# The Fourier half of an encoder kernel in tiles of 128 by 128 alone

## Chip, cores, metric

The kernel runs on one core of a Trainium2 chip. The metric is the device time of one execution in microseconds. Matrix products run on TensorE (PE), elementwise work on VectorE (DVE), ScalarE (ACT) and GpSimd (POOL); loads and stores are issued from SyncE's queue (SP).

## What is computed

Two layers of an encoder, on one sequence of 512 positions with 1024 channels, all in fp32. The reference, cut to what matters:

```python
h = rmsnorm(x, norm1[l])
p = h @ w_in[l]                       # columns: u (512) | q (512) | k (128) | v (128)
f = jnp.fft.fft2(u, axes=(1, 2), norm="ortho").real
y_f = f @ w_fourier[l] + b_fourier[l]
y_a = windowed_gqa(rope(rmsnorm(q)), rope(rmsnorm(k)), v, sink[l])   # 8 heads, |i-j| <= 128
x = x + concat([rmsnorm(y_f), rmsnorm(y_a)]) @ w_o[l]
h = rmsnorm(x, norm2[l])
up = dwconv_centred(h @ w_up[l], conv_w[l], conv_b[l])
x = x + (silu(gate) * val) @ w_down[l]
```

The edit is in the Fourier line and the product behind it.

## The kernel before

x stays on chip, transposed: eight tiles of 128 channels by 512 positions. Each layer projects q, k and v, then does the Fourier half and the attention interleaved, then the output product and the feed-forward part. In layer 0 the Fourier half runs on plain fp32 operands: one call of `mm3` is one product in the code (line 118), which the trace shows as two instructions. In layer 1 (and everywhere in the feed-forward part) each operand is split into a high and a low fp32r half, and `mm3` issues three products: high by high, low by high, high by low (lines 120 to 122). The split is `split`: ACT writes the high half (line 90), DVE the low half (line 93, or line 96 with a scale).

The Fourier half uses the symmetry of a real transform. `fold` turns 512 columns into sums (columns 0 to 256, the even plane, the last being the alternating row, sum of x[n](-1)^n) and differences (columns 257 to 511, the odd plane). So the even plane has 257 rows, in tiles of 128, 128 and 1, and the odd plane 255, in tiles of 128 and 127. The program has four steps:

- the up-projection: over eight k tiles, products into `pee[0..2]` (even) and `poo` (odd);
- stage one and stage two (`for stage in range(2)`): products with the cosine and sine tables `tabs` along channels, then along positions. The 257th row is carried apart, in `tail`, and its part is added by a product with the alternating vector `alts`, one row high (lines 589 and 591);
- between them `stage_out`, which copies the sums from PSUM into `slab` tiles and the 257th row into `tail`;
- the product with the Fourier weights, folded by `fold_wf` from `w_fold`, for four column blocks j. The weight row 256 (`wtr`, `wt`) is a product one row high.

The order of instructions on every engine is set by the framework's scheduler from its own timing of the program, so an edit of shapes may also move other work. Each engine works through its list in that order, and waits on semaphores for what the others make. In layer 0 the weights of the Fourier half are folded on DVE when they are loaded; those of layer 1 are folded and split ahead, during the feed-forward part of layer 0 (`presplit`), and fetched (`fetch`). The tables come by `load_tables`: straight into place for layer 0, and through a temporary tile of the group `m4` (five buffers) with a split for layer 1.

Among the work around the change, three names matter below. `kss` and `qs` are the rotated k and q (tiles shown as `m`), which PE transposes (lines 475 and 464). `qk3r` is a reciprocal root for twelve head pairs that POOL makes by a power (line 210), and `qknr` a DVE step on it (line 428). `ropetab` are the rotary tables, multiplied on DVE by the norm weights once a layer. L506, L510 and L518 are the scores, the masked row maximum and the transposes of the attention.

Of the kernel before, what the change touches and what calls it, by code (L numbers as in the profile page):

```python
# [16 lines left out]
P = 128  # L17
# [20 lines left out]
def encoder_kernel(tc, t):  # L38
# [34 lines left out]
    TEMPS = {"act": (1024, 8), "m4": (1024, 5), "slab": (1028, 4), "pT": (2560, 2),  # L73
# [75 lines left out]
    def presplit(l):  # L149
# [33 lines left out]
        for j in range(NF):  # L183
            jobs.append((lambda j=j: [wload(t["w_fold"][l, j], 1024, temp(1024, "m4"))], [f"f{j}"]))
# [97 lines left out]
    def load_tables(l):  # L282
        tab = []
        for i in range(2):
            if l:
                raw = temp(512, "m4")
                nc.sync.dma_start(raw, t["dft"][i])
                tab.append([cp.tile([P, 512], F32R, tag=f"t{z}{i}", name=nm("tab")) for z in "hl"])
                split(*tab[i], raw)
            else:  # L290
                tab.append([cp.tile([P, 512], F32, tag=f"th{i}", name=nm("tab"))])
                nc.sync.dma_start(tab[i][0], t["dft"][i])
        alt = cp.tile([1, 258], F32R if l else F32, tag="altr", name=nm("altr"))
        if l:
            raw = temp(258, "m4")[:1]
            nc.sync.dma_start(raw, t["alt"])
            act(alt, raw)
        else:
            nc.sync.dma_start(alt, t["alt"])
        return tab, alt  # L300
# [35 lines left out]

    def fold_wf(raw, w=None):
# [15 lines left out]
    for l in range(L):  # L353
# [205 lines left out]
        def tail_out(pe, scale):  # L559
# [4 lines left out]
        def stage_out(pe, po, scale):  # L564
            tiles = []
            if not l:
                two = temp(1028, "slab")
            for m in range(2):
                a = halves(pair("slab", 514)) if l else [two[:, m * 514:(m + 1) * 514]]
                n = P - m  # L570
# [3 lines left out]
            return tiles, tail_out(pe, scale)  # L574

        ue, ut = stage_out(pee, poo, 1.0)
        for stage in range(2):
            pe = [psum(), psum(), psum("sc")]
            po = psum()
            for m, (c0, c1) in enumerate(((0, 128), (128, 256), (256, 257))):  # L580
                o = pe[m][:c1 - c0, :258]
                for i in range(2):
                    if stage == 0:
                        mm3(o, [z[:, c0:c1] for z in ue[i]], [z[:, 0:258] for z in tabs[i]], i == 0, False)
                    else:
                        mm3(o, [z[:, c0:c1] for z in tabs[i]], [z[:, 0:258] for z in ue[i]], i == 0, False)
                for z in ut:
                    if stage == 0:
                        nc.tensor.matmul(o, z[:, c0:c1], alts, start=False, stop=z is ut[-1])
                    else:  # L590
                        nc.tensor.matmul(o, alts[:, c0:c1], z, start=False, stop=z is ut[-1])
            for m in range(2):
                n = P - m
                o = po[:n, m * 256:(m + 1) * 256]
                for i in range(2):
                    kn = P - i
                    u2 = [z[:kn, 258:514] for z in ue[i]]
                    t2_ = [z[:kn] for z in tabs[i]]
                    st = m == 0 and i == 0
                    if stage == 0:  # L600
                        mm3(o, [z[:, 1 + m * P:1 + m * P + n] for z in u2], [z[:, 256:512] for z in t2_],
                            st, i == 1, skip_group_check=True)
                    else:
                        mm3(o, [z[:, 257 + m * P:257 + m * P + n] for z in t2_], u2,
                            st, i == 1, skip_group_check=True)
# [9 lines left out]
        for j in range(NF):  # L615
# [9 lines left out]
            else:  # L625
                wt = [wtr]
                w = [fold_wf(wload(t["w_fold"][l, j], 1024), wwhole())]
# [3 lines left out]
            mm3(pu[:, :258], wt, ut, False, True)  # L631
            for i in range(2):
                kn = P - i
                mm3(pv[:, :256], [z[:kn] for z in wsum[2 + i]],
                    [z[:kn, 258:514] for z in ue[i]], i == 0, i == 1)
# [204 lines left out]
```

## Time and profile before

| | |
|---|---|
| runs | 1074.64, 1075.63, 1077.24 us; median 1075.63 |
| profiled execution | 1076.12 us, span 1074.3 us, granted clock 0.998 |
| layer 0: Fourier half and attention | about 46 to 165 us |
| layer 1: the same | about 583 to 690 us |
| HBM traffic | 131 GB/s over the span |

Times in the profile are microseconds from the first instruction. "Span" is first to last instruction; the execution's own time has 1.8 us more around it. A row of the chain or timeline gives the start, the length and what ran; "[idle <-who]" is idle time of that engine ahead of the row and what ended it. An `xN` merges N instructions of a kind. Rows of the chain follow ends, rows of the timeline starts, so the same instruction stands some tenths apart in the two. Shapes like `128*1 128x258` give the stationary operand's rows*columns and the moving operand's rows x columns.

### The profile page before, as it was taken

How to read it: one execution, taken by the hardware profiler on the slowest of the kernel's cores; microseconds unless marked ns; L12 is line 12 of the kernel's file. 1: busy time of each engine (PE TensorE's matmuls, PEld its weight loads, DVE VectorE, ACT ScalarE, POOL GpSimd, SP SyncE). 2: the span in 40 equal slices, each digit the busy share in tenths (PEclk: the TensorE clock that was granted, in tenths of full speed). 3: DMA queues.
4: the chain of work that ended last, by engine and by line, in shares of the span. 5: the costliest groups of instructions: out<-in, count | busy, mean ns of one | idle time of the engine just before them, and what ended most of it. 6: DMA issues, size and time to landing. Idle time of an engine off the chain costs nothing.

```text
span 1074.3 us, 14345 instructions
## 1 busy us (share of the span) xinstructions
PE 1060.8 (99%) x5075; PEld 881.9 (82%) x5075; DVE 737.2 (69%) x1364; ACT 510.4 (48%) x940; POOL 118.4 (11%) x171
## 2 busy tenths in 40 slices
PE   8999999999999999999999999999999999999998
PEld 7866888888888888888899887888888888888887
DVE  7856767697767777776619788387887336777632
ACT  5338755454544445455414775155554224444421
POOL 1134410000000000000001442001211000101000
PEclk9999999999999999999999999999999999999999
DMA  7242162333259932338856322423332333233241
GB/s 276 83 138 84 36 196 79 99 98 98 86 174 372 367 99 97 99 104 297 299 182 212 112 70 79 138 79 99 98 99 81 101 106 100 85 102 94 81 147 47
DMA packets 58859, 142.13 MB, mean 132 GB/s; under 512 B 6554, under 2 KB 19108, under 8 KB 58788
## 3 DMA queue, kind: packets, MB, share of 16 engines
q1 hardware_dynamic: 58788, 141.22, 40.3%
q8 instruction: 40, 0.66, 0.3%
q14 instruction: 31, 0.25, 0.1%
HBM read 118.12 MB, written 23.07 MB: 131 GB/s over the span
## 4 chain that ended last, share of the span: by engine, by line
PE 92%; DVE 4%; ACT 1%; DMA 1%; issue 1%; SPq 0%; POOL 0%; DVEq 0%; ACTq 0%
PE ps L120 27%; PE ps L122 27%; PE ps L121 27%; PE ps L118 5%; PE ps L506 2%; PE ps L518 2%; DMA wraw<-in_w_qkv_dram 1%; DVE act L93 1%; PE ps L224 1%; DVE tF L96 1%; PE ps L217 1%; DVE tA L510 0%; PE ps L464 0%; DVE tF L93 0%; DVE slab L93 0%
## 5 line engine op out<-in xcount | busy, mean ns | idle before, releaser
L90 ACT ACTIVATE whi<-wraw 128x512 fp32r<-128x512 f32 (+1 forms) x296 | 181.9, 616 | 297.8 <-PE ps L122 281.4
L93 DVE TENSOR_TENSOR wlo<-wraw,whi 128x512 fp32r<-128x512 f32 (+1 forms) x304 | 221.9, 732 | 115.5 <-ACT whi L90 113.9
L120 PE MATMUL ps<-act,whi 128*128 128x512 f32 x768 | 298.9, 390 | 0.0
L121 PE MATMUL ps<-act,wlo 128*128 128x512 f32 x768 | 298.7, 389 | 0.0
L122 PE MATMUL ps<-act,whi 128*128 128x512 f32 x768 | 298.4, 389 | 0.0
L122 PEld LDWEIGHTS ps<-act,whi 128*128 128x128 f32 x768 | 144.2, 188 | 29.9
L121 PEld LDWEIGHTS ps<-act,wlo 128*128 128x128 f32 x768 | 144.2, 188 | 29.9
L120 PEld LDWEIGHTS ps<-act,whi 128*128 128x128 f32 x768 | 144.2, 188 | 29.8
L96 DVE SCALAR_TENSOR_TENSOR tF<-tF,pb,tF 128x511 f32<-128x511 f32 x176 | 133.2, 763 | 10.6 <-ACT tF L90 8.1
L93 DVE TENSOR_TENSOR tF<-ps,rb 128x512 f32<-128x512 f32 x104 | 71.1, 689 | 76.8 <-PE ps L122 65.2
L120 PE MATMUL ps<-slab,whi 128*128 128x512 f32 (+2 forms) x212 | 83.0, 391 | 1.4 <-ACT slab L90 1.4
L121 PE MATMUL ps<-slab,wlo 128*128 128x512 f32 (+2 forms) x212 | 81.0, 382 | 0.0
L122 PE MATMUL ps<-slab,whi 128*128 128x512 f32 (+2 forms) x212 | 81.0, 384 | 0.0
L90 ACT ACTIVATE tF<-tF,pb 128x512 f32<-128x512 f32 x88 | 71.5, 815 | 8.7 <-DVE tF L93 2.3
L93 POOL TENSOR_TENSOR tF<-tF,tF 128x512 f32<-128x512 f32 x22 | 29.6, 1347 | 257.5 <-DVE tF L96 244.8
L93 DVE TENSOR_TENSOR x<-x,ps 128x512 f32<-128x512 f32 (+1 forms) x49 | 32.9, 673 | 36.3 <-PE ps L122 36.2
L509 POOL COPY tA<-nsink 128x1 f32<-128x1 f32 x64 | 15.0, 243 | 356.8 <-DMA wraw<-in_w_down_dram 321.3
L120 PE MATMUL ps<-pT,whi 128*128 128x512 f32 (+1 forms) x132 | 50.9, 385 | 0.0
L121 PE MATMUL ps<-pT,wlo 128*128 128x512 f32 (+1 forms) x132 | 50.7, 384 | 0.0
L122 PE MATMUL ps<-pT,whi 128*128 128x512 f32 (+1 forms) x132 | 50.6, 383 | 0.0
L120 PEld LDWEIGHTS ps<-slab,whi 128*128 128x128 f32 x212 | 39.8, 188 | 9.4 <-ACT slab L90 1.6
L122 PEld LDWEIGHTS ps<-slab,whi 128*128 128x128 f32 x212 | 39.8, 188 | 8.6 <-DVE nmax L510 0.2
(171 smaller groups left out, 1589.7 us busy)
## 6 DMA issues: line engine op xcount, KB each, us to landing
wraw<-in_w_up_dram SPq DMA_DIRECT2D x88, 512.0 KB, 3.5
wraw<-in_w_down_dram SPq DMA_DIRECT2D x32, 512.0 KB, 3.5
kept<-tA SPq DMA_DIRECT2D x56, 256.0 KB, 5.5
whi<-kept SPq DMA_DIRECT2D x28, 256.0 KB, 2.9
wlo<-kept SPq DMA_DIRECT2D x28, 256.0 KB, 4.2
kept<-tA SPq DMA_DIRECT2D x32, 192.0 KB, 3.3
wraw<-in_w_down_dram SPq DMA_DIRECT2D x32, 192.0 KB, 3.3
wraw<-in_w_o_dram SPq DMA_DIRECT2D x8, 512.0 KB, 3.4
```

The lines of the kernel that those rows point to most:

```text
L90: return nc.scalar.activation(out, in_, func, **kw)
L93: return (eng or nc.vector).tensor_tensor(out, a, b, op=op)
L96: return nc.vector.scalar_tensor_tensor(out=out, in0=a, scalar=s, in1=b, op0=op0, op1=op1)
L118: nc.tensor.matmul(out, a[0], b[0], start=start, stop=stop, **kw)
L120: nc.tensor.matmul(out, a[0], b[0], start=start, stop=False, **kw)
L121: nc.tensor.matmul(out, a[1], b[0], start=False, stop=False, **kw)
L122: nc.tensor.matmul(out, a[0], b[1], start=False, stop=stop, **kw)
L217: nc.tensor.matmul(pt[:, 2 * b:2 * b + 2], acc[:, b * P:(b + 1) * P], ones2, start=True, stop=True)
L224: nc.tensor.matmul(pt[:, b * P:(b + 1) * P], r[:, b:b + 1].to_broadcast([P, P]), ident, start=True, stop=True)
L506: nc.tensor.matmul(sc[:, :n], qT[p][:, e, i * P:(i + 1) * P], kT[g][:, s, j0 * P:(j1 + 1) * P], start=s == 0, stop=s == 1)
L509: nc.gpsimd.tensor_copy(pr[:, n:n + 1], nsink[:, l, h:h + 1])
L518: tr = nc.tensor.transpose(pp[:, j * P:(j + 1) * P], pr[:, j * P:(j + 1) * P], ident)
```

## The change

All operands of the Fourier half become 128 rows high and 128 columns wide, but for the weight row `wt`.

- `mm3` into `pee[2]` takes 128 stationary columns, of which the first is the alternating row, and the other 127 results are not read. The odd tiles take columns 256 to 511, so each odd tile is one row later than before, and its row 0 meets a zero.
- The alternating product is 128 rows high: `altr` is cleared and the alternating vector put in its first row, and the tail is as high as the tile, its unread rows kept. In the first `stage_out` the tail is "turned": its columns 0 to 255 and its column 256 are copied apart, by two operations.
- `stage_out` copies 257 even and 255 odd columns into a slab of 512 instead of 258 and 256 into one of 514.
- `load_tables` loads each table in two parts with the odd part shifted by a row, and clears the sine row 0; `fold_wf` builds the odd weights from the even weights' plain rows, with half the bytes loaded, and clears one row of 128.

```diff
@@ load_tables
+        rows = t["dft"].rearrange("i p c -> (i p) c")[:, 257:]
         for i in range(2):
+            raw = temp(512, "m4") if l else cp.tile([P, 512], F32, tag=f"th{i}", name=nm("tab"))
+            nc.sync.dma_start(raw[:, :257], t["dft"][i, :, :257])
+            if i == 0:
+                nc.vector.memset(raw[:1, 257:512], 0.0)
+                nc.sync.dma_start(raw[1:16, 257:512], rows[:15])
+                nc.sync.dma_start(raw[16:, 257:512], rows[15:P - 1])
+            else:
+                nc.sync.dma_start(raw[:, 257:512], rows[P - 1:2 * P - 1])
             if l:
-                raw = temp(512, "m4")
-                nc.sync.dma_start(raw, t["dft"][i])
...
-        alt = cp.tile([1, 258], F32R if l else F32, tag="altr", name=nm("altr"))
+        raw = temp(258, "m4") if l else cp.tile([P, 258], F32, tag="altr", name=nm("altr"))
+        nc.vector.memset(raw, 0.0)
+        nc.sync.dma_start(raw[:1], t["alt"])
...
@@ fold_wf (load_wf loads the first 256 columns of each half of w_fold, 256 KB)
-        tt(w[:, :256], raw[:, :256], raw[:, 512:768], ALU.add)
-        tt(w[:, 256:], raw[:, 256:512], raw[:, 768:], ALU.subtract)
+        tt(w[:, :256], raw[:, :256], raw[:, 256:512], ALU.add)
+        tt(w[:, 256:], raw[:, :256], raw[:, 256:512], ALU.subtract)
+        nc.vector.memset(w[:1, 256:384], 0.0)
@@ up-projection
-                for m, (c0, c1) in enumerate(((0, 128), (128, 256), (256, 257))):
-                    mm3(pee[m][:c1 - c0, :258], [z[:, c0:c1] for z in h], we, st, sp_)
-                mm3(poo[:, 0:256], [z[:, 257:385] for z in h], wo, st, sp_, skip_group_check=True)
-                mm3(poo[:127, 256:512], [z[:, 385:512] for z in h], wo, False, sp_, skip_group_check=True)
+                for m in range(3):
+                    mm3(pee[m][:, :258], [z[:, m * P:(m + 1) * P] for z in h], we, st, sp_)
+                for m in range(2):
+                    mm3(poo[:, m * 256:(m + 1) * 256], [z[:, 256 + m * P:384 + m * P] for z in h], wo,
+                        st and m == 0, sp_, skip_group_check=True)
@@ tail_out
-            b = halves(tp.tile([1, 2, 258], F32R if l else F32, tag="tail", name=nm("tail"), bufs=2))[:1 + l]
-            put(b, pe[2][:1, :258], scale)
+            b = halves(tp.tile([P, 2, 258], F32R if l else F32, tag="tail", name=nm("tail"), bufs=2))[:1 + l]
+            if turned:
+                put([z[:, 1:257] for z in b], pe[2][:, :256], scale)
+                put([z[:, :1] for z in b], pe[2][:, 256:257], scale)
+            else:
+                put(b, pe[2][:, :258], scale)
@@ stage_out
-                put([z[:, :258] for z in a], pe[m][:, :258], scale)
-                put([z[:n, 258:514] for z in a], po[:n, m * 256:(m + 1) * 256], scale)
+                put([z[:, :257] for z in a], pe[m][:, :257], scale)
+                put([z[:, 257:] for z in a], po[:, m * 256 + 1:(m + 1) * 256], scale)
@@ stages (the odd products likewise)
-            for m, (c0, c1) in enumerate(((0, 128), (128, 256), (256, 257))):
-                o = pe[m][:c1 - c0, :258]
+            for m in range(3):
+                o = pe[m][:, :258]
...
                 for z in ut:
                     if stage == 0:
-                        nc.tensor.matmul(o, z[:, c0:c1], alts, start=False, stop=z is ut[-1])
+                        c0 = (1, 1 + P, 0)[m]
+                        nc.tensor.matmul(o, z[:, c0:c0 + P], alts, start=False, stop=z is ut[-1])
                     else:
-                        nc.tensor.matmul(o, alts[:, c0:c1], z, start=False, stop=z is ut[-1])
+                        nc.tensor.matmul(o, alts[:, :P], z, start=False, stop=z is ut[-1])
@@ Fourier weights
-            mm3(pu[:, :258], wt, ut, False, True)
+            mm3(pu[:, :258], wt, [z[:1] for z in ut], False, True)
```

The number of products on PE is the same. Their order moves in places. On PE in layer 0, at the seam of stage one and stage two (`tab` first is stage one, `slab` first stage two; L475, or L492 after, are the transposes of k, of which `m_93` is head 0). Before:

```order
L118 MATMUL ps_698<-tab_506,slab_688 127x256
L118 MATMUL ps_698<-tab_508,slab_688 127x256
L475 MATMUL ps_545<-ident,m_93_530 128x128 x4
L475 MATMUL ps_551<-ident,m_93_530 128x128 x4
L118 MATMUL ps_921<-slab_712,tab_506 128x258
L118 MATMUL ps_921<-slab_712,tab_508 128x258
```

And after:

```order
L118 MATMUL ps_704<-tab_511,slab_693 128x256
L492 MATMUL ps_550<-ident,m_93_535 128x128 x4
L118 MATMUL ps_927<-slab_718,tab_506 128x258
L118 MATMUL ps_928<-slab_718,tab_506 128x258
L492 MATMUL ps_556<-ident,m_93_535 128x128 x4
L118 MATMUL ps_927<-slab_718,tab_511 128x258
```

Two products of stage two now stand between the transposes of the high half of k's head 0 and those of its low half.

On DVE at the same place, behind the step on POOL's power (`m_93` and `m_94` are the low halves of k, `wlo` a weight of the output product). Before:

```order
L428 TENSOR_SCALAR qknr_733<-qk3r_730 128x24
L93 TENSOR_TENSOR wlo_1455<-wraw_1452,whi_1454 128x512
L93 TENSOR_TENSOR m_93_530<-act_513,m_93_530 128x4x128
L93 TENSOR_TENSOR ropetab_5422<-ropetab_5422,pb 128x256 x4
L93 TENSOR_TENSOR m_94_533<-act_513,m_94_533 128x4x128
```

And after:

```order
L445 TENSOR_SCALAR qknr_739<-qk3r_736 128x24
L357 MEMSET whi_1132 1x128
L93 TENSOR_TENSOR wlo_1465<-wraw_1462,whi_1464 128x512
L93 TENSOR_TENSOR ropetab_5441<-ropetab_5441,pb 128x256 x4
L357 MEMSET whi_1156 1x128
L93 TENSOR_TENSOR m_93_535<-act_518,m_93_535 128x4x128
```

The low half of k's head 0 moved behind the four rotary products, and two memsets of `fold_wf` stand ahead of it.

On PE in layer 1, stage one (`ps_5704` and `ps_5705` are the first two even tiles, `ps_5706` the third; the second product of each with `altr` takes the tail's low half). Before:

```order
L121 MATMUL ps_5706<-tab_1860,slab_5696 1x258
L122 MATMUL ps_5706<-tab_1861,slab_5696 1x258
L589 MATMUL ps_5706<-altr_1864,tail_5701 1x258
L464 MATMUL ps_5487<-ident,m_1239_5457 128x128 x4
L589 MATMUL ps_5704<-altr_1864,tail_5701 128x258
L589 MATMUL ps_5705<-altr_1864,tail_5701 128x258
L464 MATMUL ps_5493<-ident,m_1239_5457 128x128 x4
L589 MATMUL ps_5706<-altr_1864,tail_5701 1x258
```

And after, with `ps_5725`, `ps_5726` and `ps_5727` for the three tiles:

```order
L481 MATMUL ps_5506<-ident,m_1239_5476 128x128 x4
L612 MATMUL ps_5725<-altr_1881,tail_5720 128x258
L612 MATMUL ps_5726<-altr_1881,tail_5720 128x258
L121 MATMUL ps_5727<-tab_1867,slab_5710 128x258
L122 MATMUL ps_5727<-tab_1868,slab_5710 128x258
L481 MATMUL ps_5512<-ident,m_1239_5476 128x128 x4
L120 MATMUL ps_5727<-tab_1874,slab_5715 128x258
```

The products with the tail's low half moved ahead of six products of the third tile.

More of the change, by code (lines that the diff above doesn't have):

```diff
@@ L290, in load_tables @@
             else:
-                tab.append([cp.tile([P, 512], F32, tag=f"th{i}", name=nm("tab"))])
-                nc.sync.dma_start(tab[i][0], t["dft"][i])
-        alt = cp.tile([1, 258], F32R if l else F32, tag="altr", name=nm("altr"))
+                tab.append([raw])
+        raw = temp(258, "m4") if l else cp.tile([P, 258], F32, tag="altr", name=nm("altr"))
+        nc.vector.memset(raw, 0.0)
+        nc.sync.dma_start(raw[:1], t["alt"])
+        alt = raw
         if l:
-            raw = temp(258, "m4")[:1]
-            nc.sync.dma_start(raw, t["alt"])
+            alt = cp.tile([P, 258], F32R, tag="altr", name=nm("altr"))
             act(alt, raw)
-        else:
-            nc.sync.dma_start(alt, t["alt"])
         return tab, alt
```

49 lines of the change are left out of this document (20 added, 29 removed).

## The prediction

> **What bounds the kernel now.** I read the page first, then the chain of work that ended last through the two Fourier parts, then the timeline where a wait ends. The page's span, busy row, clock row and chain by engine:
>
> ```profile
> span 1074.3 us, 14345 instructions
> ...
> PE 1060.8 (99%) x5075; PEld 881.9 (82%) x5075; DVE 737.2 (69%) x1364; ACT 510.4 (48%) x940; POOL 118.4 (11%) x171
> ...
> PEclk9999999999999999999999999999999999999999
> ...
> PE 92%; DVE 4%; ACT 1%; DMA 1%; issue 1%; SPq 0%; POOL 0%; DVEq 0%; ACTq 0%
> ```
>
> The reader is to see that PE carries 92% of the chain at a full clock, so time that leaves PE's stream is worth something wherever no other engine ends a wait. The edit touches two stretches: layer 0 from 46 to 93 us and layer 1 from 583 to 617 us. The chain in layer 0 (start, length, what; L118 is one plain fp32 product, L589 and L591 the alternating row's):
>
> ```profile
> 46.39 22.62 PE ps L118 x92
> 69.02 1.58 PE ps L589 x6
> 70.60 1.93 PE ps L118 x8
> 72.53 0.88 PE ps L475 x8
> ...
> 75.15 1.06 PE ps L591 x4
> 76.21 1.93 PE ps L118 x8
> ...
> 79.02 2.61 PE ps L118 x12
> ...
> 93.50 0.52 PE ps L591 x2
> ```
>
> The row at 79.02 holds only full shapes: 2.61/12 = 0.2175 us each. At that rate the row at 76.21, which follows products one row high, should take 1.74 and takes 1.93: leaving a narrow shape costs 0.19. The row at 93.50, one narrow shape after another, should take 0.435 and takes 0.52: 0.085 for a change of shape. So PE pays for the changes between full and narrow, not for the narrow product. A round trip into one column and back costs 0.09 + 0.19 = 0.28.
>
> In layer 1 the operands are fp32r, and there it depends on the kind of narrowness. The timeline (start, length, engine, line, rows*columns of the stationary operand) shows products with one stationary column, and then a full one:
>
> ```profile
> 584.41 0.28 PE L120 MATMUL ps<-whi,slab 128*1 128x258 f32 x1
> ...
> 584.64 0.28 PE L122 MATMUL ps<-wlo,slab 128*1 128x258 f32 x1
> 584.76 0.28 PE L120 MATMUL ps<-whi,slab 128*128 128x256 f32 x1
> ```
>
> The starts from 584.41 to 584.76 are three steps of 0.12 us: no price. One row high it costs again, in the chain:
>
> ```profile
> 598.82 0.32 PE ps L589
> 599.13 0.32 PE ps L120
> 599.45 0.12 PE ps L121
> ...
> 616.33 0.33 PE ps L591 x2
> 616.66 0.31 PE ps L122
> ```
>
> A product is 0.12; the one-row product and the first one after it are 0.32 each.
>
> **The change, part by part.**
>
> *Shapes in layer 0.* The number of products stays; 128x258 replaces 1x258 and 128x256 replaces 127x256, at the same 0.2175. Removed are the changes of shape: seven round trips in the up-projection (7 x 0.28 = 1.96), 0.37 in stage one up to 69.02 (two entries and one return), 0.275 (69.02 against 6 x 0.2175), 0.19 (70.60), 0.38 (75.15 and 76.21), and about 0.3 at 93.50 with the edges on its two sides. The sum is 3.48 us. The long row is 22.62 - 20.01 = 2.61 over its rate; 0.28 beyond my 2.33 I leave to PE's restart at 46.39. The one-row product with the alternating weight row (wt, wtr) stays narrow, and I take nothing there.
>
> The Trainium skill, in TensorEngine Tiling (Array Packing), section Key Properties, says that changing the tiling mode drains TensorE. The fp32 rows and the one-row fp32r rows agree with it, at 0.09 to 0.2 us a change; the fp32r rows with one column, 0.12 us apart on both sides of the change, do not. By the rule the twelve one-column groups of layer 1's up-projection would pay too, 12 x 0.28 = 3.4 us more to be won; the sum here goes by the rows.
>
> *What stops the gain in layer 0.* The changed DVE order puts the four products of the next layer's rotary tables ahead of the split of k, all of it behind one instruction that waits for POOL:
>
> ```profile
> 57.83 10.63 POOL L210 TENSOR_TENSOR qk3r<-qk3v,mhalf 128x24 f32<-128x24 f32 x1 [10.53 <-DVE qk3v L209]
> ...
> 68.49 0.18 DVE L428 TENSOR_SCALAR qknr<-qk3r 128x24 f32<-128x24 f32 x1 [4.05 <-POOL qk3r L210]
> 68.58 0.68 DVE L93 TENSOR_TENSOR wlo<-wraw,whi 128x512 fp32r<-128x512 f32 x1
> ...
> 69.79 1.42 DVE L93 TENSOR_TENSOR ropetab<-ropetab,pb 128x256 f32<-128x256 f32 x4
> ...
> 72.37 1.04 PE L475 MATMUL ps<-ident,m 128*128 128x128 f32 x8
> ```
>
> DVE sits idle 4.05 us for the power on POOL, which PE does not influence: DVE feeds it, and the work ahead of it on DVE is the same. After the change k's low half follows 68.49 by 0.09, a memset 0.06, the wlo 0.61, the tables 1.34, a memset 0.06 and itself 0.68 (as the wlo, of the same size): ready at 71.33. PE's first k transposes come at 72.37 - (1.96 + 0.37 + 0.275 + 0.19) = 69.58; 0.44 for four transposes (half the row at 72.53) and 0.87 for two stage-two products of two instructions each, moved in between, bring it to the low half at 70.89. It waits 0.44 us. From there to the end of stage two nothing new is late: all is shifted together. Layer 0 keeps 3.48 - 0.44 = 3.0 us.
>
> *Shapes in layer 1.* From 598.82 to 602.72 ten chain rows are longer than their rate, together 1.5 us; from 606.94 to 616.66 six, together 1.0. Whether that is kept is decided by the same power, now for layer 1:
>
> ```profile
> 600.87 0.18 DVE L428 TENSOR_SCALAR qknr<-qk3r 128x24 f32<-128x24 f32 x1 [3.38 <-POOL qk3r L210]
> 600.96 0.41 DVE L96 SCALAR_TENSOR_TENSOR tail<-ps,tail 1x258 fp32r<-1x258 f32 x1
> ...
> 601.42 0.50 PE L589 MATMUL ps<-altr,tail 1*128 1x258 f32 x2
> ...
> 602.64 0.39 PE L120 MATMUL ps<-tab,slab 128*128 128x256 f32 x1
> ```
>
> The alternating row's low half is written behind the wait, ready at 601.37, and PE takes it at 601.42, just in time. Six of the ten rows, 0.9 us, lie ahead of that point, and the new order moves six products of the third tile, 0.72 us, behind it: PE is there 1.6 us early and stands until 601.4 whatever it saved. Then come nine products at 0.12 and four transposes at 0.11, 1.52 us, so the odd products start at 602.9, 0.25 later than 602.64. Stage one therefore gives nothing and loses 0.25. Of stage two's 1.0 I take half. The busy time of that stretch says why:
>
> ```profile
> 594.00:620.00 26.00, 25.82 (x185) 21.26 (x183) 17.98 (x55) 20.96 (x55) 11.74 (x13) 1.00 0.25 80
> ```
>
> (PE, weight loads, DVE, ACT, POOL.) ACT is busy 20.96 of 26 us; the transposes of q stand between the products and wait for its copies out of PSUM. The bounds are 1.0 kept or none. Layer 1 gives 0.25.
>
> *Tails, memsets, DMAs.* A tail is now written at full height, and the turned one, once in each layer, in two operations instead of one. The nearest full rows:
>
> ```profile
> L90 ACT ACTIVATE slab<-ps 128x258 f32<-128x258 f32 x6 | 2.3, 386 | 17.2 <-PE ps L118 14.6 <-PE ps L591 1.6 <-PE ps L589 0.9
> ...
> L90 ACT ACTIVATE tail<-ps 1x258 f32<-1x258 f32 x3 | 1.1, 371 | 0.3
> ...
> L259 DVE MEMSET sq<- 128x512 f32 x1 | 0.5, 485 | 0.9 <-PEq L825 0.9
> L271 DVE MEMSET mhalf<- 128x1 f32 x1 | 0.1, 59 | 0.0
> ```
>
> That is 386 against 371 ns for the same number of elements in a row; the extra one-column piece lies on ACT and DVE beside PE. Each memset is between 0.06 and 0.49 us; the eight of one row by 128 and two of one row by 255 are nearest the lower, the two of 128x258 about 0.27. The two in k's path are in the 71.33 above; the others run while PE is fed. At the start the tables now take five transfers ahead of the second column half's weights, where two, the alternating row and a weight row stood. What hides a later landing:
>
> ```profile
> 19.02 1.44 ACT L90 ACTIVATE whi<-wraw 128x384 fp32r<-128x384 f32 x3 [0.36 <-DMA wraw<-in_w_qkv_dram]
> ...
> 21.73 0.69 DVE L93 TENSOR_TENSOR acc<-acc,sq 128x512 f32<-128x512 f32 x1
> ...
> 23.81 0.95 PE L217 MATMUL ps<-ones,acc 128*128 128x2 f32 x8
> ```
>
> These weights delay PE only by way of the sum of squares, done at 22.42 and needed at 23.81: 1.4 us of cover, beyond which each microsecond counts. The folded weights come as 256 KB instead of 512 KB, off the chain both times.
>
> *Sum.* -3.0 - 0.25 = -3.25 us on the profiled execution (1076.12 us, of which 1074.3 is the span). The median of the runs, 1075.63, lies 0.49 below it, so I forecast 1075.63 - 3.25 = 1072.4 us.
>
> **The rivals.**
>
> *All of it is kept.* Nothing but PE matters in either layer: 3.48 + 2.5 = 5.98 us, 1069.6. For it speaks PE's 92%; against it the two idles of DVE on POOL, 4.05 and 3.38 us, which do not move with PE.
>
> *Every change of shape costs.* The twelve one-column fp32r groups of layer 1's up-projection pay 0.28 each where the timeline does not show it; with all else kept 3.4 us more go, 1066.2. The 0.12 us steps at 584.41 speak against it. It is what the drain rule of the Trainium skill, named above, would make of them.
>
> *Hidden.* The wait for the power is longer than I reckon, or the attention that follows (the page's chain leaves PE for DVE and ACT in 5%) ends at its own time. In layer 0 the gain is gone if k's low half comes 3 us later than 71.33, or if the softmax of the first head pair, which ACT and DVE share, takes back 3 us. What is left is 0 to 2 us: 1074.7 as its middle.
>
> *Slower.* The tables of layer 1 are now cleared by DVE memsets that need a buffer which transposes of q free; before, only SP's queue waited for it:
>
> ```profile
> 90.45 0.17 DVE L514 RECIPROCAL den<-den 128x1 f32<-128x1 f32 x1 [0.92 <-ACT tA L90]
> ...
> 90.57 0.24 SPq L296 DMA_DIRECT2D m<-in_alt_dram  x1
> ...
> 91.61 0.68 DVE L510 CUSTOM_DVE_ANT_0 tA<-ps,pb,nsink 128x384 f32<-128x384 f32 x1 [0.99 <-PE ps L518]
> ```
>
> The buffer came free by 90.57, and DVE's next softmax step only at 91.61, so the memset has 1.04 us of room. Behind it stand a reciprocal and two softmax steps, which POOL and PE wait for. It decides if the new order frees the buffer more than 1.04 us later, 1 us for 1 us; the whole is slower by over 0.2% from 1.04 + 3.25 + 2.15 = 6.4 us on. At 8 us late: 1075.63 - 3.25 + 6.96 = 1079.3.
>
> **How the numbers follow.** Two tenths of a per cent, 2.15 us, is about what a measurement of this kernel can tell from no change: below 1073.5 is faster, above 1077.8 slower. The forecast (1070.5 to 1073.5) has 0.53, all kept 0.14, every change costs 0.02, hidden 0.24, slower 0.07. So faster 0.69, same 0.24, slower 0.07. The range runs from all kept, 1069.4 with rounding, to the original time, 1075.6; outside lie the case in which every change costs, slower, and about a third of hidden, together 0.17.
>
> **What would show it.** In the changed profile layer 0's up-projection and first stage should stand as one L118 row at 0.2175 each, and the one-row products of L589 and L591 at the rate of their neighbours in both layers. PE should wait about half a microsecond for k's low half, with the DVE idle before the qknr step still some 4 us. The first L506 of layer 0 should start near 80 us instead of 82.75. In layer 1 an idle PE of over a microsecond should end with the tail's low half. I am wrong if fp32 products of full height after one another still show 0.31 us steps, if the first L506 is not earlier, or if layer 1 keeps its 2.5.

## The result, and the profile after

| | median | runs |
|---|---|---|
| before | 1075.14 us | 1074.41 to 1077.24 (6 runs) |
| after | 1067.49 us | 1066.47 to 1067.96 (6 runs) |
| ratio | 0.9925 | 95% interval 0.9912 to 0.9937 |

The change saves 7.65 us, where 3.25 were forecast and the range ended at 6.2. The profiled execution took 1066.93 us, of which the span is 1065.1. The page after, its span, busy row, clock row and chain by engine:

```profile
span 1065.1 us, 14369 instructions
...
PE 1049.8 (99%) x5075; PEld 888.2 (83%) x5075; DVE 737.3 (69%) x1377; ACT 509.5 (48%) x942; POOL 117.9 (11%) x171
...
PEclk9999999999999999999999999999999999999999
...
PE 90%; DVE 5%; POOL 2%; ACT 1%; issue 1%; DVEq 0%; ACTq 0%
```

PE has the same 5075 instructions and is busy 11.0 us less. To see where, I cut the program at instructions that both kernels have and took the difference of each stretch. In some executions PE has half its clock for a few microseconds at the start: from 20 to 30 us the granted clock is 0.88 in the profiled execution of before and 1.00 in that of after. In the profiled executions of this study the first L118 comes anywhere from 44.45 to 47.62 us. So I count from it on (46.39 before, 44.90 after).

| stretch | before | after | difference |
|---|---|---|---|
| layer 0, Fourier and attention | 46.39 to 207.24 | 44.90 to 201.91 | -3.84 |
| layer 0, feed-forward | 207.24 to 552.26 | 201.91 to 544.37 | -2.56 |
| layer 1, Fourier and attention | 552.26 to 732.42 | 544.37 to 725.51 | +0.98 |
| layer 1, feed-forward, to the end | 732.42 to 1074.31 | 725.51 to 1065.06 | -2.34 |

So 4.9 us come from the two feed-forward stretches, which have none of the edited products. The busy times by stretch, of before and then of after (length, PE, weight loads, DVE, ACT, POOL):

```profile
207.24:552.26 345.02, 345.02 (x1523) 284.66 (x1521) 248.63 (x398) 168.29 (x265) 1.40 (x6) 1.00 0.53 179
732.42:1074.31 341.89, 338.60 (x1517) 279.67 (x1515) 219.14 (x294) 140.32 (x213) 29.64 (x22) 1.00 0.30 94
```

```profile
201.91:544.37 342.46, 342.46 (x1523) 284.70 (x1521) 248.82 (x402) 167.31 (x265) 1.55 (x6) 1.00 0.54 177
725.51:1065.06 339.55, 336.44 (x1517) 279.76 (x1515) 216.82 (x294) 140.12 (x213) 30.48 (x22) 1.00 0.31 95
```

In layer 0 PE is never idle there, in both kernels, at the full clock (1.00), with 1523 instructions, so some of them take less time after the change. Which ones, the groups by operation tell (count, busy time, mean ns of one), of before:

```profile
L120 PE MATMUL ps<-act,whi 128*128 128x512 f32 x768 | 298.9, 390 | 0.0
...
L122 PE MATMUL ps<-slab,whi 128*128 128x512 f32 x188 | 74.1, 397 | 0.0
...
L120 PE MATMUL ps<-pT,whi 128*128 128x512 f32 x124 | 48.6, 392 | 0.0
...
L120 PE MATMUL ps<-m,whi 128*128 128x512 f32 x93 | 36.7, 395 | 0.0
```

and of after:

```profile
L120 PE MATMUL ps<-act,whi 128*128 128x512 f32 x768 | 298.9, 390 | 0.0
...
L122 PE MATMUL ps<-slab,whi 128*128 128x512 f32 x188 | 73.2, 392 | 0.0
...
L120 PE MATMUL ps<-pT,whi 128*128 128x512 f32 x124 | 48.2, 389 | 0.0
...
L120 PE MATMUL ps<-m,whi 128*128 128x512 f32 x93 | 36.2, 389 | 0.0
```

Products that read act are unchanged. Those that read slab, pT or m (the tiles of m4) were 3 to 6 ns longer before. After the change pT and m take what act takes; slab, 64 of whose 188 products lie in the attention stretches, keeps a mean of 392. The cleaner measure is the step from the start of one product to the start of the next. In the feed-forward of layer 0 it is 233.3, 228.9 and 232.7 ns before, and 226.7 for all three after. Over 192, 192 and 144 products that makes 1.3 + 0.4 + 0.9 = 2.6 us, the whole of layer 0's 2.56.

One line of the diff, which the excerpt ahead of the prediction leaves out, touches these buffers. With rows of 512 instead of 514 columns the slab buffers are four elements shorter:

```
-    TEMPS = {"act": (1024, 8), "m4": (1024, 5), "slab": (1028, 4), "pT": (2560, 2),
+    TEMPS = {"act": (1024, 8), "m4": (1024, 5), "slab": (1024, 4), "pT": (2560, 2),
```

Buffers are laid out one after another, so this moves the starts of slab and of what lies behind it. In bytes modulo 256, from the built programs:

| | whi, wlo | act | pT | slab (four buffers) | m4 |
|---|---|---|---|---|---|
| before | 192 | 192 | 192 | 192, 224, 0, 32 | 64 |
| after | 192 | 192 | 192 | 192 | 192 |

That was the theory for the experiments: PE is slower where a moving operand does not start level with the weights.

The theory as it stands leaves one row of the table open: pT is level with the weights in both kernels, and yet its products took 228.9 ns before. The order of the products answers this. In each group of before, pT follows the slab products. In layer 0 the first five pT products behind them have steps of about 231, 236, 228, 233 and 231 ns, and the other seven 226 or 227. One slab buffer is level too (192), and its three products, which stand behind others off level, take 230, 236 and 228 ns. So the slow pace outlasts the last product that is off level, by five products here and by seven in layer 1, and a level product can be slow because of those ahead of it.

### The profile page after: what moved, and what is told of

It is laid out like the page before. It is cut to its first block, busy times and chain, and to the rows that moved or that the text cites. A ratio compares the mean times of both kernels' runs of the same rounds, so it can differ in the third digit from the quotient of the medians.

```text
span 1065.1 us, 14369 instructions
## 1 busy us (share of the span) xinstructions
PE 1049.8 (99%) x5075; PEld 888.2 (83%) x5075; DVE 737.3 (69%) x1377; ACT 509.5 (48%) x942; POOL 117.9 (11%) x171
## 4 chain that ended last, share of the span: by engine, by line
PE 90%; DVE 5%; POOL 2%; ACT 1%; issue 1%; DVEq 0%; ACTq 0%
PE ps L120 28%; PE ps L121 27%; PE ps L122 27%; PE ps L118 3%; POOL qk3r L210 2%; PE ps L535 2%; PE ps L523 1%; DVE act L93 1%; DVE slab L93 1%; PE ps L224 1%; DVE tF L96 1%; PE ps L217 1%; DVE qkssq L440 1%; DVE tF L93 0%; DVE whi L93 0%
## 5 line engine op out<-in xcount | busy, mean ns | idle before, releaser
L120 PE MATMUL ps<-act,whi 128*128 128x512 f32 x768 | 298.9, 390 | 0.0
L93 DVE TENSOR_TENSOR wlo<-wraw,whi 128x512 fp32r<-128x512 f32 (+1 forms) x304 | 219.3, 724 | 98.4 <-ACT whi L90 95.5
L120 PEld LDWEIGHTS ps<-act,whi 128*128 128x128 f32 x768 | 144.2, 188 | 29.9
L120 PE MATMUL ps<-slab,whi 128*128 128x512 f32 (+2 forms) x212 | 81.8, 386 | 1.6 <-ACT slab L90 1.6
L122 PE MATMUL ps<-slab,whi 128*128 128x512 f32 (+2 forms) x212 | 79.6, 379 | 0.0
L120 PE MATMUL ps<-pT,whi 128*128 128x512 f32 (+1 forms) x132 | 50.5, 383 | 0.0
L120 PEld LDWEIGHTS ps<-slab,whi 128*128 128x128 f32 x212 | 39.9, 188 | 8.7 <-ACT slab L90 1.9
L527 DVE CUSTOM_DVE_ANT_0 tA<-ps,pb,nsink 128x256 f32<-128x256 f32 (+1 forms) x64 | 38.1, 601 | 11.8 <-PE ps L523 5.5
```

The source lines that it names most:

```text
L93: return (eng or nc.vector).tensor_tensor(out, a, b, op=op)
L120: nc.tensor.matmul(out, a[0], b[0], start=start, stop=False, **kw)
L122: nc.tensor.matmul(out, a[0], b[1], start=False, stop=stop, **kw)
L527: nc.vector.tensor_tensor_reduce(out=pr[:, :n], in0=sc[:, :n], in1=mask[:, m0:m0 + n], scale=qs_scale[p][:, i, e:e + 1], scalar=nsink[:, l ...
```

## Experiments on where the buffers start

**The slab buffers long again.** In the changed kernel:

```
-"slab": (1024, 4)
+"slab": (1028, 4)
```

> The changed kernel, with the slab buffers 1028 elements long again, as before the change; nothing is laid out differently inside them and the order on every engine is the same. Theory A (where the buffers start): the 4.9 us that the two feed-forward stretches gave beyond my sum come from the shorter slab buffers, which move the starts of slab and m4 buffers. Then the products with slab, m and pT as moving operand take 233, 232.6 and 229 ns again instead of 226.7, the feed-forward is 2.6 us longer in layer 0 and 2.3 us in layer 1, and the time is about 1072.4 us. Rival B (something else in the change did it: transfers of half the size, full-height tails, or a luckier run): the steps stay at 226.7 ns and the time at 1067.5 us.

Measured: 1073.32 us (1072.22 to 1074.91), 0.9978 of before (0.9969 to 0.9987). The steps are 233.3, 232.7 and 228.9 ns again, and the feed-forward rows repeat those of before to the hundredth in PE's busy time:

```profile
204.32:549.34 345.02, 345.02 (x1522) 284.73 (x1521) 249.28 (x402) 167.66 (x265) 1.92 (x6) 1.00 0.52 176
730.73:1072.45 341.72, 338.60 (x1517) 279.66 (x1515) 219.12 (x294) 140.33 (x213) 29.63 (x22) 1.00 0.31 94
```

Theory A holds, B falls. The one number is worth 5.8 us by the two medians as they stand, and 5.2 when each is first set against the runs of before taken with it (7.65 us saved against 2.48). By the stretches 4.7 of it lie in the feed-forward, 0.25 in the attention stretch of layer 1 (181.39 us against 181.14), and 0.33 in that of layer 0, behind the first scores. The attention stretches have a share because output projections read slab too: 64 of the 188 products in each slab row. What is left to everything else that was changed is 0.22%, 1.4 to 3.3 us.

**All moving operands shifted against the weights**, by 128, 256 and 64 bytes, and weights and operands shifted together:

```
-"sq": (512, 2)}          (128 bytes)      -"sq": (512, 2)}          (256 bytes)
+"sq": (528, 2)}                           +"sq": (544, 2)}
-"sq": (512, 2)}          (64 bytes)       -wp.tile([P, 1024], F32, tag="wraw", ...)
+"sq": (520, 2)}                           +wp.tile([P, 1056], F32, tag="wraw", ...)[:, :1024]
```

> The changed kernel with its first two temporary buffers (sq) 64 bytes longer each, so that all moving operands of the feed-forward (act, slab, pT, m) start 128 bytes later and the weights (whi, wlo) do not; the order is the same. By the built program before's m4 buffers stood 128 bytes off the weights, counted modulo 2048 bytes, and after's stand level with them. Theory A1 (the distance between moving operand and weights modulo 2048 counts) and A2 (the moving operand's own address modulo 256 counts): the act products too take about 232.6 ns, some 2750 products of 128x512 x 5.9 ns = 16 us more, 1083.7 us. Theory A3 (only buffers that start off a multiple of 64 bytes are slow, and delay their neighbours): no change, 1067.5 us, since all stand on a multiple of 64.

> The changed kernel with the three raw weight buffers 128 bytes longer each, so that split weights and temporaries all start 384 bytes later together: the moving operands' own addresses modulo 256 become those of before's m4 buffers, their distance to the weights stays zero modulo 2048. Theory A1 (distance to the weights): no change, 226.7 ns a product, 1067.5 us. Theory A2 (own address modulo 256): all 128x512 products at about 232.6 ns, some 16 us more, 1083.7 us. Theory A3 (off a multiple of 64): no change.

> The changed kernel with both sq buffers 128 bytes longer, so that all moving operands start 256 bytes off the weights instead of level with them (128 bytes made every product with 512 moving columns 232.4 ns instead of 226.7). The order is the same. If the distance counts modulo 256 bytes the steps are 226.7 ns again and the time 1067.5 us; if the period is 512 bytes or more, they are slow, at 228 to 240 ns, and the time is between 1071 and 1090 us. The four column blocks of a weight tile lie 512 bytes apart and are all at 226.7, so the period is no more than 512.

> The changed kernel with both sq buffers 32 bytes longer, so that all moving operands start 64 bytes off the weights (0 and 256 bytes off gave 226.7 ns a product of 512 columns, 128 bytes 232.4). The order is the same. If any distance that is not a multiple of 256 costs, the steps are between 228 and 237 ns, as with the slab buffers at 32, 64 and 96 bytes, and the time is between 1071 and 1090 us; if only half the period (128) costs, 226.7 ns and 1067.5 us.

| moving operand against weights | step of a 512-column product | time |
|---|---|---|
| level (after) | 226.7 ns | 1067.49 us |
| level, both moved by 384 bytes | 226.7 ns | 1067.83 us (1066.44 to 1068.43) |
| 256 bytes off | 226.7 ns | 1068.15 us (one run) |
| 64 bytes off | 228.9 ns | 1075.5 us (one run) |
| 128 bytes off | 232.4 ns | 1087.39 us (1087.13 to 1087.48) |

The act products, untouched in every kernel above, are slow as soon as they lie 128 bytes off, here beside m (L120's groups in that kernel):

```profile
L120 PE MATMUL ps<-act,whi 128*128 128x512 f32 x768 | 303.0, 395 | 0.0
...
L120 PE MATMUL ps<-m,whi 128*128 128x512 f32 x93 | 36.7, 395 | 0.0
```

The steps in the table are means over the three products of a group. At 128 bytes off the three are alike (232.2 to 232.6 ns); at 64 bytes off they are 231.7, 225.9 and 229.1 ns, so the product with wlo is not slow there.

The 128 bytes cost 19.9 us where 16 were expected. The expectation took some 2750 products; the groups count 3519 of 512 columns, and 3519 x 5.7 ns are 20.1 us. In the profiled execution 16.6 us lie in the feed-forward and 2.1 in the attention stretches, which I had not counted. So it is the distance (A1), modulo 256 bytes as far as the distances tried can tell. It is not the operand's own address (A2): moved together with the weights by 384 bytes, nothing changes. Nor does standing on a multiple of 64 suffice (A3).

**A gap between whi and wlo.** The small memset is the only other difference.

```
 hi = wp.tile([P, 512], F32R, tag="whi", ...)
+gap = wp.tile([P, 32], F32, tag="gap", bufs=1)      (once, 128 bytes)
 lo = wp.tile([P, 512], F32R, tag="wlo", ...)
```

> The changed kernel with a buffer of 128 bytes between the whi and the wlo buffers: wlo and all moving operands stay level with one another, whi lies 128 bytes off both. The order is the same, but for one small memset at the start. If what counts is the distance between a product's moving operand and its stationary operand (or the next one's, which is loaded meanwhile), the two of three products with whi are slow and those with wlo less so, unevenly by place in the three: between 1073 and 1087 us. If it were the distance to buffers of other engines, nothing changes: 1067.5 us.

Measured: 1090.66 us (one run); in the feed-forward of layer 0 the steps of the three products of a group are 232.5, 234.9 and 232.6 ns. All three are slow, the one with wlo, which is level, most of all. The moving operands lie level with wlo here and only whi does not, so the weights' place counts as much as that of the moving operand. A simple rule (a product is slow if its own stationary operand is off) would have left the product with wlo fast. As with pT above, a level product between others off level is slow. Which reads meet inside PE stays open.

**The constants moved level too**, on the best version below: the pa tile 80 elements long instead of 72, and the alternating row's 314 instead of 258.

> The kernel of the run beside it, with its constants moved by 32 and 256 bytes, so that the Fourier tables, the alternating row and the values (vz) start level with the other operands modulo 256 bytes; they lay 32 bytes off (160 against 192). The order is the same. In layer 1 some 100 products of 256 or 384 columns with vz and 54 with a table's high half are touched, at 2 to 6 ns each, and in part they lie beside waits: 0.3 to 0.6 us less, 1064.2 us, if 32 bytes off costs as 128 does. If it costs nothing, or is hidden: the same as the run beside it.

Measured: 1065.72 us against 1065.05 without. From the first L118 to the end it is 1017.04 against 1016.99 us in the profiled executions. Nothing is gained: these constants at 32 bytes off, with products of 256 and 384 columns, cost nothing that shows here.

## Experiments on the shapes and the waits

**One-column tiles back** in six of the eight k of the up-projection:

```
-mm3(pee[m][:, :258], [z[:, m * P:(m + 1) * P] for z in h], we, st, sp_)
+c = P if k in (0, KT - 1) or m < 2 else 1
+mm3(pee[m][:c, :258], [z[:, m * P:m * P + c] for z in h], we, st, sp_)
```

> The changed kernel with the third tile of the up-projection one stationary column wide again for six of its eight k, in both layers; the output is the same. By the fp32 rows (0.09 in, 0.19 out) layer 0 pays 6 x 0.28 = 1.7 us in its up-projection, of which the 0.43 us that PE stood waiting for k's low half hide a part: the first score product comes 1.2 us later, at 79.7 us instead of 78.5. In layer 1 the fp32r rows say nothing is paid, the up-projection's steps stay at 118 ns and the total is about 1068.8 us. Rival (each change drains, fp32r too): 6 x 0.28 = 1.7 us more in layer 1's up-projection, of which the wait of 1.57 us for the tail's low half may hide most; there the steps around a narrow product read 0.2 to 0.3 us instead of 0.12.

Measured: 1069.26 us (1068.03 to 1069.57). The chain's long row in layer 0, first in the run with long slab buffers (all shapes full), then with narrow tiles:

```profile
47.62 19.37 PE ps L118 x88
```

```profile
46.01 21.09 PE ps L118 x88
```

The same 88 products take 1.72 us more, for 1.68 expected. In layer 1 the stretch from the first sum of squares to the first transposes of k is 42.91 us against 42.99. The one-column fp32r products cost nothing there; the rival falls. By the Trainium skill, TensorEngine Tiling (Array Packing), section Key Properties, a change of tiling mode drains TensorE. The built program gives the one-column products tiles of 128 by 32 among those of 128 by 128, so the mode does change; in fp32r this run shows no price for it.

**The alternating row one row high again:**

```
-nc.tensor.matmul(o, z[:, c0:c0 + P], alts, ...)      -nc.tensor.matmul(o, alts[:, :P], z, ...)
+nc.tensor.matmul(o, z[:1, c0:c0 + P], alts[:1], ...) +nc.tensor.matmul(o, alts[:1, :P], z[:1], ...)
```

> The changed kernel with the products of the alternating row one row high again (one stationary row and one moving row, output still 128 rows), in both stages and both layers; the order is the same. By my step on shapes layer 0 pays 0.37 + 0.275 + 0.19 + 0.38 + 0.3 = 1.5 us less what the wait for k's low half hides, so 1.1 to 1.5 us by the first transpose of the probabilities. In layer 1 stage one's 0.9 us lie behind PE's wait of 1.57 us for the tail and cost nothing; of stage two's 1.0 us between none and all. Together 1068.6 to 1070.0 us. Rival: stage two too is hidden (ACT sets its end) and layer 0's wait takes all it can, 1068.3 us.

Measured: 1073.81 us, with two executions at 1069.7 and eight at 1072.8 to 1074.6. In layer 0 the stretch from the first L118 to the first transposes of the probabilities is 42.23 us against 40.68 with full rows and no wait for k (the run with long slab buffers): 1.55 for 1.5 expected. The two lower executions lie in the range expected; the eight others I had not foreseen. Layer 1's stage one in one of them, by stretch (granted clock third from the end), and PE's timeline ahead of it:

```profile
590.00:596.50 6.50, 5.62 (x38) 4.32 (x36) 3.06 (x9) 3.09 (x9) 5.51 (x1) 1.00 0.50 170
596.50:603.40 6.90, 6.90 (x30) 6.41 (x30) 3.08 (x8) 3.62 (x9) 0.00 (x0) 0.51 0.00 0
603.40:606.00 2.60, 2.60 (x22) 2.56 (x22) 1.82 (x4) 2.33 (x4) 0.00 (x0) 0.98 0.03 6
```

```profile
594.29 0.38 PE L612 MATMUL ps<-altr,tail 1*128 1x258 f32 x1
594.60 0.66 PE L481 MATMUL ps<-ident,m 128*128 128x128 f32 x4
596.11 0.50 PE L612 MATMUL ps<-altr,tail 1*128 1x258 f32 x2 [0.85 <-DVE tail L96]
```

After a wait of 0.85 us beside one-row products PE has half its clock for 6.9 us, which costs about 3.4 (half of it, an estimate).

**One-row products without that wait.** The edit above and the next one together.

> The alternating row's products one row high again, as in the run of that name, and the qknr step behind the low halves, so that PE does not wait for the tail. In the run with one-row products, eight of ten executions had half the clock for some 7 us in stage one of layer 1 (596.4 to 603.4 us), and took 3 to 5 us longer than the other two, at 1069.7 us. Theory A (it takes the wait of about a microsecond beside the one-row products to lower the clock): the drop is gone or rarer, and the time is 1065.7 plus 1.5 (layer 0) plus 0 to 1.0 (stage two of layer 1), about 1067.8 us at a clock of 0.998 to 1.000. Rival B (the one-row products alone do it): the clock still falls in most executions and the median is above 1070 us.

Measured: 1070.37 us (1068.90 to 1071.88). The profiled execution holds the clock (third from the end) from layer 1's first transposes of k to its first transposes of the probabilities:

```profile
588.55:607.68 19.13, 17.94 (x129) 15.57 (x128) 11.89 (x36) 15.39 (x39) 8.19 (x6) 1.00 0.16 57
```

So of A the part on the clock holds in the execution that was profiled. The four others show 0.997 and 0.998, which executions of before show too, so their clocks do not tell; a median above 1070 us was what B forecast. A's sum does not hold. Against the next kernel, which differs in the alternating row alone, the profiled execution loses 1.91 us in layer 0 (1.5 expected) and 1.85 in layer 1 (0 to 1.0 expected), 1.45 of these between its first sum of squares and its first transposes of the probabilities (62.13 us against 60.68). Of that 0.69 lies ahead of the first scores (51.87 us against 51.18): without the wait, stage one has nothing to hide them behind. The loss explains most of the median, 1070.37 against 1065.68.

**DVE's step behind the power moved.** The qknr step is issued behind k's low half in layer 0 and behind the tail's in layer 1 (lows holds those two instructions):

```
-nc.vector.tensor_scalar(nr, r, ...)
+with tc.issue_after(lows[-1]) if n == 3 else nullcontext():
+    nc.vector.tensor_scalar(nr, r, ...)
```

> The changed kernel with one instruction on DVE moved in each layer: the qknr step, which waits for POOL's power over the q heads, stands behind k's low half in layer 0 and behind the tail's last low half in layer 1, instead of ahead of them. Nothing else moves on any engine. In the changed kernel PE stood 0.43 us for k's low half (layer 0; 0 in runs whose first L118 comes a microsecond later) and 1.57 us for the tail (layer 1). Theory A (DVE's order behind the power costs what PE waits): both waits go, the first scores of layer 1 come 1.5 us sooner after the layer's first sum of squares (52.39 us in the changed kernel), and the time falls by 1.6 to 2.0 us to about 1065.7 us. Rival B (stage two of layer 1 is set by ACT, which is busy 9.2 of 9.5 us there and lets PE wait 1.1 to 2.8 us for a slab): what the tail gains there is waited for at the slab, and the time falls by 0.5 us at most, 1067.0 us.

Measured: 1065.68 us (1064.57 to 1066.19), 0.9904 of before. What PE waits for in layer 1 in the changed kernel:

```profile
593.54 0.51 PE L612 MATMUL ps<-altr,tail 128*128 128x258 f32 x2 [1.57 <-DVE tail L96]
601.47 0.39 PE L120 MATMUL ps<-slab,tab 128*128 128x258 f32 x1 [1.15 <-ACT slab L90]
```

and with the step moved:

```profile
592.44 0.39 PE L121 MATMUL ps<-tab,slab 128*128 128x258 f32 x1 [0.51 <-DVE slab L96]
599.17 0.39 PE L120 MATMUL ps<-slab,tab 128*128 128x258 f32 x1 [1.15 <-ACT slab L90]
```

The 1.57 us are gone; the next low half in line, slab's, is 0.51 late. The first scores come 51.19 us after layer 1's first sum of squares instead of 52.39, and 32.93 after the first L118 in layer 0 instead of 33.58. That is 1.2 and 0.65 us, in all the 1.8 by which the medians differ. A holds.

**And ACT's copy ahead of the table load** (highs holds the copies of the high halves). In the changed kernel ACT does this in front of the copy that PE waits for until 601.47:

```profile
599.25 1.28 ACT L90 ACT_TABLE_LOAD   x1
600.55 0.51 ACT L90 ACTIVATE tA<-tA,nmax 128x257 f32<-128x257 f32 x1
...
601.06 0.36 ACT L90 ACTIVATE slab<-ps 128x255 fp32r<-128x255 f32 x1
```

The edit:

```
-act(pr[:, :n + 1], pr[:, :n + 1], AF.Exp, ...)
+with tc.issue_after(highs[-2]) if l and p == 3 and e + i == 0 else nullcontext():
+    act(pr[:, :n + 1], pr[:, :n + 1], AF.Exp, ...)
```

> The changed kernel with the qknr step behind the low halves (as in the run before, which gave 1065.7 us) and, on ACT in layer 1, the copy of stage one's last odd half into slab (0.39 us) ahead of the load of the exponential's table and the first exponential, not behind them. In the changed kernel that copy starts at 601.06 us though its products were done by 597, and PE stands 1.15 us for it at the start of stage two's second block. Theory A (ACT's order costs what PE waits): another 0.8 to 1.2 us, 1064.7 us. Rival B (the first softmax, now 0.4 us later, or the copies of q set the end of stage two instead): no more than 0.3 us, 1065.5 us.

Measured: 1065.05 us (1063.96 to 1066.06), 0.9907 of before (0.9892 to 0.9923). ACT now, around the copy:

```profile
597.19 0.39 ACT L90 ACTIVATE slab<-ps 128x255 fp32r<-128x255 f32 x1
597.60 1.28 ACT L90 ACT_TABLE_LOAD   x1
...
603.06 0.40 ACT L90 ACTIVATE slab<-ps 128x255 fp32r<-128x255 f32 x1
```

The wait of 1.15 us is gone, and one of 0.55 us for a later copy of q stands in its place (at 603.33). From the first L118 to the end the profiled execution is 1016.99 us against 1018.29, 1.3 less; the medians differ by 0.6, and at one clock (1.000) the executions are at 1064.0 against 1064.6 and 1065.2. This is the fastest version by its median. Whether it beats the run before it, their intervals against before do not tell: they overlap, and by that ratio the run before it is ahead (0.9904).

## Why the prediction was wrong

**The step that failed: the sum counts the two edited stretches alone.** All the rest of the program, the two feed-forward stretches above all, stands in it at nothing, and no reason is given. What the runs show in its place is the length of the slab buffers: one line of the diff, which the prediction does not mention and which is worth 5.2 to 5.8 us, 4.7 of them in the feed-forward. With the buffers long again the changed kernel takes 1073.32 us, inside the range forecast. The groups of before had the sign of it in plain sight: 395 ns for the first product of a group that reads m (line 120), 390 for the one that reads act. I looked at the edited stretches alone, and asked of no other group why its mean was what it was.

**The rest, by itself, came out near the forecast, by two errors of opposite sign.** With the slab buffers long again the kernel is at -0.22% (0.13 to 0.31), and from the first L118 to the end its profiled execution is 3.09 us below before's. The forecast was 3.25. In that execution layer 0's Fourier and attention are 4.15 us shorter than before, where 3.0 were forecast, and layer 1's are 1.23 longer, where 0.25 shorter were forecast.

- *Shapes in layer 0.* Up to the first transposes of k 2.88 us are saved (25.98 to 23.10 from the first L118), for 1.96 + 0.37 + 0.275 + 0.19 = 2.80 predicted. The prices of a change of shape stand: 1.72 for 1.68 and 1.55 for 1.5 when put back.
- *The wait behind POOL's power in layer 0.* Predicted 0.44, and seen:

```profile
57.89 9.36 POOL L210 TENSOR_TENSOR qk3r<-qk3v,mhalf 128x24 f32<-128x24 f32 x1 [10.53 <-DVE qk3v L209]
...
67.28 0.18 DVE L445 TENSOR_SCALAR qknr<-qk3r 128x24 f32<-128x24 f32 x1 [2.56 <-POOL qk3r L210]
...
70.20 0.66 PE L492 MATMUL ps<-ident,m 128*128 128x128 f32 x4 [0.43 <-DVE m L93]
```

  It depends on how quick the start was: in the run 256 bytes off, whose first L118 comes at 46.71 us instead of 44.90, PE reaches k after its low half is done and does not wait. That the size agrees is in part chance: PE started 1.5 us earlier than before, and the power took 9.36 us, not 10.63, so DVE stood 2.56 us for it and not some 4. The first scores come at 78.48 us, for "near 80", 1.5 of it by the earlier start.
- *Layer 0 behind the first scores.* I counted 0.3 there, and 1.06 came (3.84 less 2.78). Of it 0.56 lies before the first transposes of the probabilities. Of the 0.50 behind them 0.33 go when the slab buffers are long again, and belong to the buffers' place.
- *Layer 1.* Predicted -0.25, measured +0.98 (+1.23 with the slab buffers long again). This is the second term that failed. The wait of PE for the tail is there with 1.57 us (forecast: over one, 1.6 early). The half of stage two's 1.0 us that I kept was not kept. The odd half of slab, computed by 597, stood on ACT behind the table load and the first exponential until 601.06, and PE stood 1.15 us for it. I had named ACT (20.96 of 26 us busy) and the copies of q as the limit, but no instruction. The two runs with moved steps show both waits to come from the order on DVE and ACT: with the DVE step moved, layer 1's stretch is 1.2 us shorter than in the changed kernel, and with the copy moved as well 2.5 us.
- *Tails, memsets, transfers and the slower rival.* They were put at nothing but for the two memsets in k's path, and nothing more of them appears: no wait of PE in the changed kernel names a transfer or a memset.

**The rivals.** That every change of shape costs gave 1066.2 us, the nearest number, by a mechanism that the run with one-column tiles excludes. The right time for the wrong reason would have been no better forecast. Its price was also counted too high: the up-projection of layer 1 has eight one-column groups, not twelve; the other four stand in the two stages.

## What to carry to other kernels

Read the groups of one operation against one another, also where the edit does not reach: the same product at 390 ns from one buffer and 395 from another is a question, and a buffer's length is part of a change even if nobody reads the elements it loses. Lay out operands that PE streams so that they start level with the weights, modulo 256 bytes, and compare sizes at equal layout before a difference is put down to the algorithm. Where PE waits for a step that itself needs no long input, look at what stands ahead of it in its engine's queue: moving one DVE step in each layer gave 1.8 us.

## What the runs showed of the hardware

- In these fp32r streams a product of 512 columns takes 226.7 ns from start to start with its moving operand level with the weights modulo 256 bytes, 228.9 at 64 bytes off and 232.4 at 128. With whi alone 128 bytes off it is 233.3 on average. A level product behind others that are off level is slow too: five to seven products behind the last of them were. By the Trainium skill, SBUF — State Buffer, section SBUF: two separate sides, only the port pair that DVE and GpSimd share causes contention among engine reads, and its table gives the weight loads a read port of their own. Neither leads one to expect what these runs show: where the weights lie against the moving operand changes the pace by up to 2.9%. Whether the two reads meet at a port is not shown.
- One-column stationary operands cost nothing between full ones in fp32r (0.12 us steps), and 0.29 us a round trip in plain fp32 (1.72 us for six).
- One-row products beside a wait of 0.85 us halved PE's clock for 6.9 us in the profiled execution, and by their times in seven others of ten; full-height products beside a wait of 1.57 us did not. The Trainium skill, TensorE: Matmul & The Clock Gate, section What's actually happening, describes a free-running window of 3.4 us; two of them are 6.8, which agrees. The profiled execution of the kernel with one-row products and without the wait keeps its clock, and so does the changed kernel with the wait and without one-row products, so here it took both; why the height counts is not shown.
